# A FiLM layer on one core: loads on one queue, whole-slab stores, a narrow transposing matmul, compute in program order

## The chip, the cores and the metric

One core of a Trainium2 chip. The metric is device time in microseconds (us) of one execution. The profile's span is the time from the core's first to its last instruction; it is some 1.8 us shorter than the time (82.6 against 84.35 us in the profiled run of the kernel before). An execution counts as slow when it is more than 1.5% above the fastest of the same kernel. Comparisons use the others, the fast ones.

## The reference, cut to what matters

```python
x            : float32 [32, 512, 256]      # 16.78 MB in, 16.78 MB out
conditioning : float32 [32, 64]
gamma_proj, beta_proj : float32 [64, 256]

gamma = conditioning @ gamma_proj
beta  = conditioning @ beta_proj
return x * (1 + gamma[:, None, :]) + beta[:, None, :]
```

The arithmetic is two operations per element. The 33.69 MB of traffic cannot be reduced, since input and output are float32.

## The kernel before

x is cut into four slabs of 4 MB. A slab has eight batches on 128 partitions; each partition holds 32 rows of 1 KB, 32 KB in one contiguous run of memory. The kernel keeps all four slabs on the chip at once (four tiles of 32 KB per partition), so no buffer is reused. A matmul with a repeated identity turns the conditioning over and repeats each batch 16 times; a second matmul per slab gives gamma and beta for each partition. VectorE then handles 11 of every 16 rows and GpSimd 5, each with a multiply and an add, and each group of 16 rows is stored as soon as it is done.

```python
    cond_s = consts.tile([batch, cond_dim], f32)
    nc.scalar.dma_start(out=cond_s, in_=conditioning)          # small loads: ScalarE's queue
    gbproj = consts.tile([cond_dim, 2 * dim], f32)
    nc.scalar.dma_start(out=gbproj[:, :dim], in_=gamma_proj)
    nc.scalar.dma_start(out=gbproj[:, dim:], in_=beta_proj)
    for s in range(SLABS):                                     # slab loads: SP's queue
        ...
        for n in LOADS.get(s, [ROWS]):                         # slab 0: 8 + 24 rows, others 32
            nc.sync.dma_start(out=xs[:, r : r + n, :], in_=x_v[s, :, r : r + n, :])
    ...                                                        # rident: identity, each column 16 times
    nc.tensor.matmul(cond_T_p, lhsT=cond_s, rhs=rident, start=True, stop=True)   # 512 columns
    nc.vector.tensor_copy(out=cond_T, in_=cond_T_p)
    ...                                                        # per slab: gb_p = cond_T.T @ gbproj, copy to gb_s
    for s in range(SLABS):
        ...
        for r0 in range(0, ROWS, GROUP):                       # GROUP = 16, ON_DVE = 11
            ...
            nc.vector.scalar_tensor_tensor(out=v, in0=rows(g_p, nv), scalar=1.0, in1=v,
                                           op0=ALU.add, op1=ALU.mult)
            nc.gpsimd.tensor_tensor(out=w, in0=w, in1=rows(g_s, nw), op=ALU.mult)
            nc.vector.tensor_add(out=v, in0=v, in1=rows(b_p, nv))
            nc.gpsimd.tensor_tensor(out=w, in0=w, in1=rows(b_s, nw), op=ALU.add)
            nc.scalar.dma_start(out=o_v[s, :, r0 : r0 + GROUP, :],
                                in_=xs[:, r0 : r0 + GROUP, :])
```

## Time and profile before

| | kernel before |
|---|---|
| time, median of the first 3 runs | 85.82 us (84.4, 85.82, 86.3) |
| time of the profiled run, its span | 84.35 us, 82.6 us |
| VectorE busy, GpSimd busy | 49.9 us (60%), 46.2 us (56%) |
| DMA queues' packets, share of 16 engines' span | 48.6% + 48.0% |
| first multiply on VectorE, last compute ends | 17.5 us, 66.6 us |

The prediction below shows the lines of these views. In them PE is TensorE (PEld its weight loads), DVE is VectorE, ACT is ScalarE, POOL is GpSimd and SP is SyncE; q1 and q10 are the two DMA queues, and a packet is one contiguous run that one of the 16 DMA engines moves (the stores of the kernel before left 1024 records of 16 KB), or the 4 B record of a completion, 16 for each transfer. Three more things help in reading them. The DMA row gives the busy share of 40 equal slices of the span in tenths, 9 for full. Rows of the table by stretches end with the DMA share and the GB/s of that stretch; a packet is counted where it starts, so a share can pass 1.00 (1.30 from 4 to 6 us in the kernel before). And the chain of waits ends at the last instruction of an engine (66.6 us in the kernel before); a store that runs after it (until 81.4 us) is not part of it.

### The profile page before, as it was taken

How to read it: one execution, taken by the hardware profiler on the slowest of the kernel's cores; microseconds unless marked ns; L12 is line 12 of the kernel's file. 1: busy time of each engine (PE TensorE's matmuls, PEld its weight loads, DVE VectorE, ACT ScalarE, POOL GpSimd, SP SyncE). 2: the span in 40 equal slices, each digit the busy share in tenths (PEclk: the TensorE clock that was granted, in tenths of full speed). 3: DMA queues.
4: the chain of work that ended last, by engine and by line, in shares of the span. 5: the costliest groups of instructions: out<-in, count | busy, mean ns of one | idle time of the engine just before them, and what ended most of it. 6: DMA issues, size and time to landing. Idle time of an engine off the chain costs nothing.

```text
span 82.6 us, 156 instructions
## 1 busy us (share of the span) xinstructions
PE 9.1 (11%) x10; PEld 2.8 (3%) x10; DVE 49.9 (60%) x18; ACT 3.9 (5%) x9; POOL 46.2 (56%) x22
## 2 busy tenths in 40 slices
PE   0080000899600000000000000000000000000000
PEld 0100000443000000000000000000000000000000
DVE  2011000059999999999999999999999920000000
ACT  0600000034400000000000000000000000000000
POOL 2000000069999999999999999999995000000000
DMA  3899999969969989998889979899999999999992
GB/s 56 337 508 397 389 397 524 460 302 508 508 270 492 508 381 381 413 476 381 381 381 556 460 302 460 381 468 421 429 452 389 468 421 421 460 389 452 437 421 87
DMA packets 2080, 33.69 MB, mean 408 GB/s; under 512 B 288, under 2 KB 416, under 8 KB 416
## 3 DMA queue, kind: packets, MB, share of 16 engines
q1 hardware_dynamic: 720, 16.78, 48.6%
q10 hardware_dynamic: 1360, 16.92, 48.0%
HBM read 16.92 MB, written 16.78 MB: 408 GB/s over the span
## 4 chain that ended last, share of the span: by engine, by line
DVE 49%; DMA 16%; issue 11%; PE 2%; ACTq 1%; ACT 1%
DVE xs L100 30%; DVE xs L103 19%; DMA gbproj<-in_beta_proj_dram 16%; PE gb_p L79 2%; ACTq L50 1%; ACTq L48 0%; ACT gb_s L82 0%; ACT gb_s L85 0%
## 5 line engine op out<-in xcount | busy, mean ns | idle before, releaser
L102 POOL TENSOR_TENSOR xs<-xs,gb_s 128x1280 f32<-128x1280 f32 x8 | 23.0, 2895 | 16.2 <-ACT gb_s L82 16.2
L100 DVE SCALAR_TENSOR_TENSOR xs<-gb_p,xs 128x2816 f32<-128x2816 f32 x8 | 24.7, 3083 | 10.9 <-ACT gb_s L85 10.9
L103 DVE TENSOR_TENSOR xs<-xs,gb_p 128x2816 f32<-128x2816 f32 x8 | 24.7, 3086 | 0.3
L104 POOL TENSOR_TENSOR xs<-xs,gb_s 128x1280 f32<-128x1280 f32 x8 | 23.0, 2893 | 0.0
L79 PE MATMUL gb_p<-gbproj,cond_T 64*128 64x512 f32 x8 | 7.2, 1074 | 8.9 <-DMA gbproj<-in_beta_proj_dram 8.9
L74 DVE COPY cond_T<-cond_T_p 64x512 f32<-64x512 f32 x1 | 0.7, 683 | 4.3 <-PE cond_T_p L72 4.3
L79 PEld LDWEIGHTS gb_p<-gbproj,cond_T 64*128 64x128 f32 x8 | 2.5, 328 | 13.7 <-issue 13.7
L72 PE MATMUL cond_T_p<-rident,cond_s 32*64 32x512 f32 x2 | 1.9, 1065 | 3.9 <-DMA cond_s<-in_conditioning_dram 3.9
L82 ACT ACTIVATE gb_s<-gb_p 128x256 f32<-128x256 f32 x4 | 1.5, 383 | 16.4 <-PE gb_p L79 16.4
L85 ACT COPY gb_s<-gb_p 128x256 f32<-128x256 f32 x4 | 1.5, 367 | 0.0
L82 ACT ACT_TABLE_LOAD x1 | 1.3, 1283 | 2.4 <-issue 2.4
L67 DVE COPY rident<-ident 32x512 f32<-32x512 f32 x1 | 0.4, 416 | 1.2 <-POOL ident masks.py:199 1.2
L72 PEld LDWEIGHTS cond_T_p<-rident,cond_s 32*64 32x64 f32 x2 | 0.3, 202 | 3.9 <-issue 3.9
masks.py:197 POOL MEMSET ident<- 32x32 f32 x1 | 0.1, 114 | 0.3 <-POOLq L121 0.3
masks.py:199 POOL TENSOR_SCALAR_AFFINE_SELECT ident<-ident 32x32 f32<-32x32 f32 x1 | 0.2, 202 | 0.1
L121 POOL MEMSET const-float32-0.0<- 128x1 f32 x1 | 0.1, 103 | 0.2 <-issue 0.2
L121 POOL MEMSET const-bfloat16-1.0<- 128x1 bf16 x1 | 0.1, 106 | 0.0
L121 POOL MEMSET const-uint8-127<- 128x1 uint8 x1 | 0.1, 106 | 0.0
L121 POOL MEMSET const-float32-1.0<- 128x1 f32 x1 | 0.1, 103 | 0.0
## 6 DMA issues: line engine op xcount, KB each, us to landing
out_dram<-xs ACTq DMA_DIRECT2D x8, 2048.0 KB, 18.2
xs<-in_x_dram SPq DMA_DIRECT2D x3, 4096.0 KB, 32.9
xs<-in_x_dram SPq DMA_DIRECT2D x1, 3072.0 KB, 12.2
xs<-in_x_dram SPq DMA_DIRECT2D x1, 1024.0 KB, 4.6
gbproj<-in_gamma_proj_dram ACTq DMA_DIRECT2D x1, 64.0 KB, 9.1
gbproj<-in_beta_proj_dram ACTq DMA_DIRECT2D x1, 64.0 KB, 12.9
cond_s<-in_conditioning_dram ACTq DMA_DIRECT2D x1, 8.0 KB, 3.0
```

The lines of the kernel that those rows point to most:

```text
L50: nc.scalar.dma_start(out=gbproj[:, :dim], in_=gamma_proj)
L67: nc.vector.tensor_copy(out=rident.rearrange("p (b g) -> p b g", g=REP), in_=ident.to_broadcast([batch, batch, REP]),)
L72: nc.tensor.matmul(cond_T_p, lhsT=cond_s, rhs=rident, start=True, stop=True)
L74: nc.vector.tensor_copy(out=cond_T, in_=cond_T_p)
L79: nc.tensor.matmul(p_t, lhsT=cond_T[:, s * P : (s + 1) * P], rhs=gbproj, start=True, stop=True)
L82: nc.scalar.activation(out=s_t[:, :dim], in_=p_t[:, :dim], func=mybir.ActivationFunctionType.Identity, bias=1.0, scale=1.0)
L85: nc.scalar.copy(out=s_t[:, dim:], in_=p_t[:, dim:])
L100: nc.vector.scalar_tensor_tensor(out=v, in0=rows(g_p, nv), scalar=1.0, in1=v, op0=ALU.add, op1=ALU.mult)
L102: nc.gpsimd.tensor_tensor(out=w, in0=w, in1=rows(g_s, nw), op=ALU.mult)
L103: nc.vector.tensor_add(out=v, in0=v, in1=rows(b_p, nv))
L104: nc.gpsimd.tensor_tensor(out=w, in0=w, in1=rows(b_s, nw), op=ALU.add)
L121: nc = _bacc.Bacc("TRN2", target_bir_lowering=False, num_devices=1)
```

## The change: its intent, and the diff

The small loads leave ScalarE's queue and go behind slab 0 in SP's, so that they take no turns with it. Each slab is stored in one transfer with runs of 32 KB, as long as those of the loads. The transposing matmul works on 32 columns, and the repetition moves to a broadcasting copy per slab. The compute loop is issued in program order.

```diff
-    nc.scalar.dma_start(out=cond_s, in_=conditioning)
-    nc.scalar.dma_start(out=gbproj[:, :dim], in_=gamma_proj)
-    nc.scalar.dma_start(out=gbproj[:, dim:], in_=beta_proj)
 ...
+    load(nc.sync, 0, 0)
+    load(nc.sync, 0, 1)
+    nc.sync.dma_start(out=cond_s, in_=conditioning)
+    nc.sync.dma_start(out=gbproj[:, :dim], in_=gamma_proj)
+    nc.sync.dma_start(out=gbproj[:, dim:], in_=beta_proj)
+    load(nc.sync, 1, 0)
+    load(nc.sync, 2, 0)
+    load(nc.sync, 3, 0)
 ...
-    cond_T_p = psum.tile([cond_dim, batch * REP], f32)
-    nc.tensor.matmul(cond_T_p, lhsT=cond_s, rhs=rident, start=True, stop=True)
-    nc.vector.tensor_copy(out=cond_T, in_=cond_T_p)
+    cond_T_p = psum.tile([cond_dim, batch], f32)
+    nc.tensor.matmul(cond_T_p, lhsT=cond_s, rhs=ident, start=True, stop=True)
     for s, sl in enumerate(slabs):
+        nc.vector.tensor_copy(
+            out=c_t.rearrange("p (b g) -> p b g", g=rep),
+            in_=cond_T_p[:, b0 : b0 + n].to_broadcast([cond_dim, n, rep]),
+        )
 ...
+    STORES = [[32], [32], [32], [32]]
+    PIECE, ON_DVE = 16, 11
+    with tc.manual_schedule():
+        for s, sl in enumerate(slabs):
             ...                                   # the four operations of each piece as before
-            nc.scalar.dma_start(out=o_v[s, :, r0 : r0 + GROUP, :],
-                                in_=xs[:, r0 : r0 + GROUP, :])
+                nc.scalar.dma_start(out=sl["dst"][:, done : done + n, :],
+                                    in_=xs[:, done : done + n, :])
```

More of the change, by code (lines that the diff above doesn't have):

```diff
@@ L28 @@
     P = 128
-    SLABS = 4
-    BS = batch // SLABS
-    REP = P // BS
-    ROWS = BS * seq // P
-    assert SLABS * BS == batch and REP * BS == P and ROWS * REP == seq
-    x_v = x.flatten_outer_dims().rearrange("(s p r) d -> s p r d", s=SLABS, p=P)
-    o_v = out.flatten_outer_dims().rearrange("(s p r) d -> s p r d", s=SLABS, p=P)
-    LOADS = {0: [8, 24]}
-    GROUP = 16
-    ON_DVE = 11
+    SLABS = [(8, [8, 24]), (8, [32]), (8, [32]), (8, [32])]
+    assert sum(n for n, _ in SLABS) == batch
+    STORES = [[32], [32], [32], [32]]
+    PIECE, ON_DVE = 16, 11
+    x_f = x.flatten_outer_dims()
+    o_f = out.flatten_outer_dims()
     consts = ctx.enter_context(tc.tile_pool(name="consts", bufs=1))
@@ L44 @@
     psum = ctx.enter_context(tc.tile_pool(name="psum", bufs=1, space=bass.MemoryType.PSUM))
+    slabs = []
+    b0 = 0
+    for s, (n, loads) in enumerate(SLABS):
+        assert P % n == 0
+        rows = n * seq // P
+        r0, r1 = b0 * seq, (b0 + n) * seq
+        slabs.append(dict(
+            n=n, b0=b0, rows=rows, loads=loads,
+            src=x_f[r0:r1, :].rearrange("(p r) d -> p r d", p=P),
+            dst=o_f[r0:r1, :].rearrange("(p r) d -> p r d", p=P),
+            xs=xpool.tile([P, rows, dim], f32, name=f"xs{s}"),
+        ))
+        b0 += n
@@ L47, with load @@
+    def load(eng, s, i):
+        sl = slabs[s]
+        r = sum(sl["loads"][:i])
+        n = sl["loads"][i]
+        eng.dma_start(out=sl["xs"][:, r : r + n, :], in_=sl["src"][:, r : r + n, :])
     cond_s = consts.tile([batch, cond_dim], f32)
-    nc.scalar.dma_start(out=cond_s, in_=conditioning)
     gbproj = consts.tile([cond_dim, 2 * dim], f32)
-    nc.scalar.dma_start(out=gbproj[:, :dim], in_=gamma_proj)
-    nc.scalar.dma_start(out=gbproj[:, dim:], in_=beta_proj)
-    slabs = []
-    for s in range(SLABS):
-        xs = xpool.tile([P, ROWS, dim], f32, name=f"xs{s}")
-        slabs.append(xs)
-        r = 0
-        for n in LOADS.get(s, [ROWS]):
-            nc.sync.dma_start(out=xs[:, r : r + n, :], in_=x_v[s, :, r : r + n, :])
-            r += n
-        assert r == ROWS
+    load(nc.sync, 0, 0)
@@ L64 @@
+    load(nc.sync, 0, 1)
[5 more added lines that the diff above has]
+    load(nc.sync, 3, 0)
     ident = consts.tile([batch, batch], f32)
     make_identity(nc, ident)
-    rident = consts.tile([batch, batch * REP], f32)
-    nc.vector.tensor_copy(
-        out=rident.rearrange("p (b g) -> p b g", g=REP),
-        in_=ident.to_broadcast([batch, batch, REP]),
-    )
@@ L71 @@
-    cond_T_p = psum.tile([cond_dim, batch * REP], f32)
-    nc.tensor.matmul(cond_T_p, lhsT=cond_s, rhs=rident, start=True, stop=True)
-    cond_T = consts.tile([cond_dim, batch * REP], f32)
-    nc.vector.tensor_copy(out=cond_T, in_=cond_T_p)
-    gb_p, gb_s = [], []
-    for s in range(SLABS):
+    gb_p, gb_s = [], []
+    cond_T_p = psum.tile([cond_dim, batch], f32)
+    nc.tensor.matmul(cond_T_p, lhsT=cond_s, rhs=ident, start=True, stop=True)
+    for s, sl in enumerate(slabs):
+        n, b0 = sl["n"], sl["b0"]
+        rep = P // n
+        c_t = consts.tile([cond_dim, P], f32, name=f"cond_T{s}")
+        nc.vector.tensor_copy(
+            out=c_t.rearrange("p (b g) -> p b g", g=rep),
+            in_=cond_T_p[:, b0 : b0 + n].to_broadcast([cond_dim, n, rep]),
+        )
@@ L78 @@
         p_t = psum.tile([P, 2 * dim], f32, name=f"gb_p{s}")
-        nc.tensor.matmul(p_t, lhsT=cond_T[:, s * P : (s + 1) * P], rhs=gbproj,
-                         start=True, stop=True)
+        nc.tensor.matmul(p_t, lhsT=c_t, rhs=gbproj, start=True, stop=True)
         s_t = consts.tile([P, 2 * dim], f32, name=f"gb_s{s}")
@@ L87, with spread @@
         gb_s.append(s_t)
-    def rows(t, n):
+    def spread(t, n):
         return bass.AP(tensor=t.tensor, offset=t.offset, ap=[t.ap[0], [0, n], t.ap[1]])
-    for s in range(SLABS):
-        xs = slabs[s]
-        g_p, b_p = gb_p[s][:, :dim], gb_p[s][:, dim:]
-        g_s, b_s = gb_s[s][:, :dim], gb_s[s][:, dim:]
-        for r0 in range(0, ROWS, GROUP):
-            v = xs[:, r0 : r0 + ON_DVE, :]
-            w = xs[:, r0 + ON_DVE : r0 + GROUP, :]
-            nv, nw = ON_DVE, GROUP - ON_DVE
-            nc.vector.scalar_tensor_tensor(out=v, in0=rows(g_p, nv), scalar=1.0, in1=v,
-                                           op0=ALU.add, op1=ALU.mult)
-            nc.gpsimd.tensor_tensor(out=w, in0=w, in1=rows(g_s, nw), op=ALU.mult)
-            nc.vector.tensor_add(out=v, in0=v, in1=rows(b_p, nv))
-            nc.gpsimd.tensor_tensor(out=w, in0=w, in1=rows(b_s, nw), op=ALU.add)
-            nc.scalar.dma_start(out=o_v[s, :, r0 : r0 + GROUP, :],
-                                in_=xs[:, r0 : r0 + GROUP, :])
+    with tc.manual_schedule():
+        for s, sl in enumerate(slabs):
+            xs = sl["xs"]
+            g_p, b_p = gb_p[s][:, :dim], gb_p[s][:, dim:]
+            g_s, b_s = gb_s[s][:, :dim], gb_s[s][:, dim:]
+            done = 0
+            for n in STORES[s]:
+                for q0 in range(done, done + n, PIECE):
+                    nv, nw = ON_DVE, PIECE - ON_DVE
+                    v = xs[:, q0 : q0 + nv, :]
+                    w = xs[:, q0 + nv : q0 + PIECE, :]
+                    nc.vector.scalar_tensor_tensor(out=v, in0=spread(g_p, nv), scalar=1.0, in1=v,
+                                                   op0=ALU.add, op1=ALU.mult)
+                    nc.gpsimd.tensor_tensor(out=w, in0=w, in1=spread(g_s, nw), op=ALU.mult)
+                    nc.vector.tensor_add(out=v, in0=v, in1=spread(b_p, nv))
+                    nc.gpsimd.tensor_tensor(out=w, in0=w, in1=spread(b_s, nw), op=ALU.add)
+                nc.scalar.dma_start(out=sl["dst"][:, done : done + n, :],
+                                    in_=xs[:, done : done + n, :])
+                done += n
+            assert done == sl["rows"]
 _INS = ['x', 'conditioning', 'gamma_proj', 'beta_proj']
```

## The prediction

> **What bounds the kernel now.** I read the head of the profile page first: busy shares, then the slices, then the queues.
>
> ```profile
> PE 9.1 (11%) x10; PEld 2.8 (3%) x10; DVE 49.9 (60%) x18; ACT 3.9 (5%) x9; POOL 46.2 (56%) x22
> ...
> DMA  3899999969969989998889979899999999999992
> ...
> q1 hardware_dynamic: 720, 16.78, 48.6%
> q10 hardware_dynamic: 1360, 16.92, 48.0%
> HBM read 16.92 MB, written 16.78 MB: 408 GB/s over the span
> ```
>
> No compute engine is above 60%. The two DMA queues together take 48.6 + 48.0 = 96.6% of the 16 DMA engines' span, 79.8 of 82.6 us, and the DMA row is full from its second slice to its last but one. The queues are told apart by bytes: q1 carries the 16.78 MB of x, and q10, the queue that ScalarE issues on, the stores and the small loads. The 2.8 us outside are the ends: by the packet records the first packet starts at 1.7 us and the last ends at 81.4 us.
>
> The chain of waits seems to say otherwise, so I read it with its last entries.
>
> ```profile
> DVE 49%; DMA 16%; issue 11%; PE 2%; ACTq 1%; ACT 1%
> ```
> ```profile
> 60.46 3.01 DVE xs L100
> 63.47 0.02 issue
> 63.49 3.09 DVE xs L103
> ```
>
> It names VectorE for half the span. But it follows back from the last compute instruction, which ends at 66.6 us. The last 16 us have no compute in them, so the chain does not explain them. The table by stretches shows what does.
>
> ```profile
> 14.60:26.00 11.40, 7.16 (x8) 2.50 (x8) 8.45 (x3) 2.59 (x8) 8.70 (x4) 1.00 0.97 420
> 26.00:50.00 24.00, 0.00 (x0) 0.00 (x0) 23.86 (x9) 0.00 (x0) 24.00 (x9) 1.00 1.00 423
> 50.00:66.00 16.00, 0.00 (x0) 0.00 (x0) 15.89 (x6) 0.00 (x0) 12.97 (x5) 1.00 1.01 434
> 66.00:80.50 14.50, 0.00 (x0) 0.00 (x0) 0.58 (x1) 0.00 (x0) 0.00 (x0) 1.00 1.00 429
> ```
>
> The last two columns are DMA share and GB/s. Loads only, the mix, and stores only, with compute beside them or without: 420 to 434 GB/s and a share of 0.97 or more in every row. **The bound is the transport of 33.69 MB**, and compute only has to hand stores over before the queue runs dry.
>
> [...] In the stretch with both kinds, 26 to 50 us, I read the two queue lines:
>
> ```profile
> q1 hardware_dynamic: 238, 6.75, 67.0%
> q10 hardware_dynamic: 224, 3.41, 33.1%
> ```
>
> Packets come nearly one for one, but a load packet is 32 KB and a store packet 16 KB, so loads get two thirds. [...]
>
> **The change, part by part.**
>
> *Stores in 32 KB runs.* Packet records: an 8 KB load takes 309 ns, a 16 KB store 611 ns, a 32 KB load 1213 ns (medians). Twice 611 is 1222, so joining two runs saves 9 ns. The 1024 store packets are 64 on each of 16 engines, 32 pairs: 32 x 9 ns = 0.29 us. Four completion packets fewer per engine at 9 ns: 0.04 us. Together **-0.3 us**, on the bounding resource.
>
> *Small loads behind slab 0.* Bytes and packets are the same; per engine some 0.5 us (8 packets of 46 ns, 2 of 18 ns, completions) move within the queue, **0 us** in transport. Now the wait for them:
>
> ```profile
> 1.72 12.90 DMA gbproj<-in_beta_proj_dram
> 14.62 0.14 issue
> 14.76 2.06 PE gb_p L79 x2
> 16.82 0.02 issue
> 16.84 0.38 ACT gb_s L82
> 17.22 0.27 ACT gb_s L85
> ```
>
> Today beta takes 12.9 us although it was issued at 1.7 us, since each little packet takes turns with a slab packet: its last data packet ends at 12.8 us, about when slab 0's do (12.75). Behind slab 0 in one queue I expect the data at about 12.9 us and the wait over at 13.5 us (conditioning's wait ended 0.7 us after its last packet), 1.1 us earlier. But conditioning now comes with it, so the transpose, hidden before, is exposed.
>
> *Narrow matmul.* Two passes of 512 columns at 1065 ns become two of 32: in proportion 0.07 us each, with fixed costs I guess 0.3 us for both. The 0.42 us copy of the repeated identity goes; the 0.68 us copy becomes four of a quarter of its width, 0.2 us each, of which one is on the path. Exposed: some 0.6 us less 0.4 us that overlaps with the wait for beta. So VectorE starts near 16.7 us instead of 17.5: **-0.8 us, off the bound**.
>
> *Program order, one store per slab.* Scheduling moves no bytes. VectorE's pace stays 6.13 us per piece (eight pieces from 17.52 to 66.58). The first store goes out after two pieces, at about 16.7 + 12.3 = 29 us instead of 25.9. Until then the load queue keeps the DMA engines full: only 13.5 of the 24 big load packets per engine had been done when the first store packet started today (29.8 us). **0 us**.
>
> Sum: -0.3 us of 82.6, or 85.82 x (82.3 / 82.6) = 85.5 us. All that could be won, ends included, is small: per engine 8 x 309 + 8 x 923.5 (24 KB packets) + 24 x 1213 + 64 x 611 ns + 0.55 us of small ones = 78.6 us, against 79.8 us taken. Even the full 1.2 us of slowed packets plus 0.3 would be 1.8%.
>
> **Rivals.**
> *A new wait for slab 3.* With equal runs, loads get half of the engines where they had two thirds. The first store was issued at 25.9 us and its packets started at 29.8; the same lag puts store packets at about 33 us after the change, with (33 - 13) / 1.27 = 15.7 big load packets done (1.27 us each in the load-only stretch). The other 8.3 alternate with stores at 1.24 + 1.21 us: the loads end at 53 us, landing 1 us later at 54; with no such lag, 56.5. VectorE wants slab 3 at 16.7 + 6 x 6.13 = 53.5 us. So I expect a stall of 0.5 to 3 us, new, and hidden if the next rival fails.
>
> *The last store comes too late.* It is 4 MB now: 8 packets x 1.213 = 9.7 us per engine, plus about 1 us from issue to first packet. The work before it ends at 81.4 - 9.7 = 71.7 us, so it may be issued as late as 70.7. VectorE would end at 16.7 + 49.1 + 0.5 to 3 = 66.3 to 68.8 us. The slack is 2 to 4 us; today it is larger, since the last store is half as long. If it were overrun by 2 us the time would be 87.5 us.
>
> *A real gain on the DMA side.* Large runs, or fewer takings of turns, could take away the slowed load packets (1.24 to 1.27 against 1.213 us) and the first slab's slow start. For it: the trace has them. Against it: they are there in loads without any small packets or stores beside them. Worth at most 1.2 us: 84.3 us.
>
> **Range and chances.** The centre is 85.5, moved to 85.3 for the third rival, which I find likelier than the second. The runs of before spread from 84.4 to 86.3, wider than every effect above, so the range is 83.9 to 86.8. Faster by 2% needs under 84.1, more than all the slack in the sum, so chiefly a lucky median: 0.13. Slower by 2% needs over 87.5, an overrun of the last store: 0.07. Within 2%: 0.80.
>
> **What would show it.** Right: queue shares again near 97% together, stretches at 420 to 434 GB/s, store packets half as many, byte shares near 50:50 where loads and stores mix, VectorE starting near 16.7 us, a wait of VectorE or GpSimd for the load of x before slab 3, and a DMA row full to the end. Wrong: empty tenths in the DMA row between two stores, a first multiply later than 18 us, a wait of over 4 us for x, or a rate clearly above 434 GB/s.

## The result, and the profile after

The changed kernel took 84.53 us (median of 6 runs, 84.45 to 84.78). The kernel before took 85.2 us (median of 6 runs, 84.4 to 86.47). A ratio is the mean time of one kernel's fast runs over that of the other's of the same rounds, so not quite the ratio of these medians: it is **1.0004, with a 95% interval of 0.9985 to 1.0024, the same**. The medians differ because three of the six runs of the kernel before were slow (85.82, 86.3, 86.47); its other three, 84.4 to 84.59, lie where the changed kernel's do.

The head of the page after the change, with busy shares, slices and queues (q1 is now every load, q10 every store):

```profile
PE 7.6 (9%) x10; PEld 2.8 (3%) x10; DVE 49.7 (60%) x20; ACT 3.9 (5%) x9; POOL 46.6 (56%) x22
...
DMA  2898989889969989979969998996998899799790
...
q1 hardware_dynamic: 928, 16.92, 49.1%
q10 hardware_dynamic: 576, 16.78, 47.0%
```

The same engines are as busy as before and the DMA row has no hole. The stores have fallen from 1024 data packets to 512, and the two shares together from 96.6 to 96.1%, which is 0.3 us of packet time, as predicted. The span did not follow: 82.7 us against 82.6.

The table by stretches after the change (engine times, then clock, DMA share and GB/s), for the same four stretches as before:

```profile
14.60:26.00 11.40, 7.00 (x8) 2.31 (x8) 9.11 (x5) 2.59 (x8) 8.87 (x4) 1.00 0.96 414
26.00:50.00 24.00, 0.00 (x0) 0.00 (x0) 23.86 (x9) 0.00 (x0) 23.68 (x9) 1.00 1.03 437
50.00:66.00 16.00, 0.00 (x0) 0.00 (x0) 15.89 (x6) 0.00 (x0) 13.52 (x5) 1.00 0.99 426
66.00:80.50 14.50, 0.00 (x0) 0.00 (x0) 0.27 (x1) 0.00 (x0) 0.00 (x0) 1.00 1.00 434
```

Each rate differs from the one before by 5 to 14 GB/s up or down, and the four stretches together moved 28.3 MB against 28.1: I read the differences as the edges of 32 KB packets, not as a new rate.

The two queues after the change, while loads and stores run side by side (33 to 50 us):

```profile
q1 hardware_dynamic: 112, 3.67, 49.9%
q10 hardware_dynamic: 112, 3.67, 49.9%
```

Packets are one for one as before, and with equal runs the bytes are too, where loads had two thirds. The chain of waits shows the start of the compute (start, length, what):

```profile
1.64 11.87 DMA cond_s<-in_conditioning_dram
...
13.64 0.40 PE cond_T_p L81 x2
...
14.06 0.29 DVE cond_T L86
...
14.40 2.09 PE gb_p L91 x2
...
17.19 3.10 DVE xs L114
```

The waits for the small loads end at 13.5 us for conditioning and at 13.9 for beta (14.6 before), but the transpose now lies open behind conditioning: 0.76 us from its first matmul to the first gb_p. The multiply starts at 17.2 us, 0.3 us earlier than before. The first store is issued at 29.6 us instead of 25.9, its packets start at 33.7, and a new wait has come, in the table of waits (in total, times, longest):

```profile
POOL xs L116 <- DMA xs<-in_x_dram: 0.8, 1, 0.8
```

It is GpSimd waiting for slab 3 at 52 us. VectorE, which is 1.2 us later there, does not wait.

### The profile page after: what moved, and what is told of

It reads as the page before. It is cut to its first block, busy times and chain, and to the rows that moved or that the text cites. A ratio compares the mean times of both kernels' runs of the same rounds, so it can differ in the third digit from the quotient of the medians.

```text
span 82.7 us, 151 instructions
## 1 busy us (share of the span) xinstructions
PE 7.6 (9%) x10; PEld 2.8 (3%) x10; DVE 49.7 (60%) x20; ACT 3.9 (5%) x9; POOL 46.6 (56%) x22
## 2 busy tenths in 40 slices
DMA packets 1504, 33.69 MB, mean 407 GB/s; under 512 B 224, under 2 KB 352, under 8 KB 352
## 4 chain that ended last, share of the span: by engine, by line
DVE 51%; DMA 14%; issue 9%; PE 3%; SPq 1%; ACT 1%
DVE xs L114 30%; DVE xs L117 21%; DMA cond_s<-in_conditioning_dram 14%; PE gb_p L91 3%; SPq L63 1%; PE cond_T_p L81 0%; ACT gb_s L93 0%; DVE cond_T L86 0%; ACT gb_s L96 0%
## 5 line engine op out<-in xcount | busy, mean ns | idle before, releaser
L86 DVE COPY cond_T<-cond_T_p 64x128 f32<-64x128 f32 x4 | 0.9, 274 | 14.1 <-PE cond_T_p L81 14.1
```

The costliest lines, as they stand in the source:

```text
L86: nc.vector.tensor_copy(out=c_t.rearrange("p (b g) -> p b g", g=rep), in_=cond_T_p[:, b0 : b0 + n].to_broadcast([cond_dim, n, rep]),)
```

## The experiments

Theory: the 33.69 MB set the time, so a part counts only if it changes what the 16 engines move, delays their first packet, or lets them run dry. Rivals: the VectorE chain that the profile names sets the end; or each packet has a fixed cost worth saving. The twelve kernels ran each beside fresh runs of the kernel before.

| run | what | median us | ratio to before (95%) |
|---|---|---|---|
| e1_copy | changed, no arithmetic on x | 84.91 | 1.0046 (1.0019 to 1.0073) |
| e2_run4k | changed, stores in 4 KB runs | 85.62 | 1.0128 (1.0106 to 1.0150) |
| e3_run1k | changed, stores in 1 KB runs | 89.4 | 1.0574 (1.0550 to 1.0597) |
| e4_st16 | changed, two 16 KB stores per slab | 84.4 | 0.9987 (0.9966 to 1.0008) |
| e5_after_d2 | changed, last store 5.9 us later | 86.2 | 1.0200 (1.0182 to 1.0218) |
| e6_after_d3 | changed, last store 8.9 us later | 89.36 | 1.0570 (1.0552 to 1.0588) |
| e7_before_d3 | before, last store 8.7 us later | 85.59 (2 of 4 slow; fast: 84.61, 84.69) | 1.0014 (0.9993 to 1.0036) |
| e8_small_act | changed, small loads first on ScalarE | 84.67 (1 of 4 slow) | 1.0013 (0.9995 to 1.0031) |
| e9_before_behind | before, small loads behind slab 0 | 84.63 | 1.0012 (0.9993 to 1.0031) |
| e10_before_sp_first | before, small loads first on SP | 86.09 | 1.0184 (1.0166 to 1.0203) |
| e11_after_again | the changed kernel | 84.66 (1 of 6 slow) | 1.0019 (0.9993 to 1.0045) |
| e12_sixteen | changed, sixteen transfers | 84.37 | 0.9979 (0.9965 to 0.9994) |

### Does compute set the end? (e1_copy)

```diff
-                for q0 in range(done, done + n, PIECE):
-                    ...                          # all four operations on x
                 nc.scalar.dma_start(out=sl["dst"][:, done : done + n, :], ...)
```

> The changed kernel with its arithmetic on x left out (result wrong on purpose); stores depend on the loads alone. Theory (transport bound, 33.69 MB[...] between a head of 1.7 us and a tail of 1.2 to 1.4 us): the span stays at 82 to 83 us, a ratio of 0.99 to 1.01 to the kernel before, although VectorE and GpSimd lose 46 to 49 us of work. Rival (the chain of waits through VectorE, half of the span, sets the end): well under 80 us.

By its packet records the kernel before moved the 33.69 MB between 1.7 and 81.4 us, at 423 GB/s, in a span of 82.6 us.

The result is wrong on purpose: x is copied. The head of its page:

```profile
span 83.0 us, 101 instructions
...
PE 7.6 (9%) x10; PEld 2.8 (3%) x10; DVE 0.9 (1%) x4; ACT 3.9 (5%) x9; POOL 0.5 (1%) x6
```

VectorE fell from 49.7 to 0.9 us and GpSimd from 46.6 to 0.5, and the kernel was not faster at all; it was 0.5% slower than the kernel before. The VectorE half of the chain of waits is worth nothing in time.

### What does a packet cost? (e2_run4k, e3_run1k, e4_st16)

```diff
-                nc.scalar.dma_start(out=sl["dst"][:, done : done + n, :],
-                                    in_=xs[:, done : done + n, :])
+                d_r = sl["dst"].rearrange("p (c two k) d -> p two c (k d)", two=2, k=RUN)   # RUN = 4 or 1
+                x_r = xs.rearrange("p (c two k) d -> p two c (k d)", two=2, k=RUN)
+                for h in range(2):
+                    nc.scalar.dma_start(out=d_r[:, h], in_=x_r[:, h])
```

> The changed kernel with each slab's store cut into two DMAs of interleaved 4 KB runs: 256 store packets per engine in place of 32. Prediction's term (9 ns of fixed cost per packet on the bounding engines): 224 x 9 ns = +2.0 us. Rival (the 9 ns in the packet records lie over the neighbouring packet and cost nothing): within 0.4 us of the changed kernel.

> The same with runs of 1 KB: 1024 store packets per engine in place of 32. Prediction's term: 992 x 9 ns = +8.9 us, over 93 us. Rival (overlapped, no cost): within 0.6 us. Something between: a cost that appears only when packets are short.

Neither theory hit. Against the changed kernel's 84.53 us, 224 more packets per engine cost 1.09 us and 992 more cost 4.87 us: **4.9 ns per packet both times**, a little over half of the 9 ns that the packet records suggested. One caution: these two kernels have sixteen transfers and the changed kernel twelve, and the last experiment shows that twelve cost 0.25 us more at the end. Adding it makes 6.0 and 5.2 ns of the two figures. The comparison free of it is between these two kernels: 89.4 - 85.62 = 3.78 us for 768 packets, again 4.9 ns. The traces agree. While stores ran alone they moved 386 GB/s in 1 KB runs (e3_run1k, 46 to 84 us) and 422 in 4 KB runs (e2_run4k, 46 to 80 us), which is 42.4 and 155.3 ns per packet on each of 16 engines. The difference, 112.9 ns for 3 KB, is 37.6 ns for each KB (the records of the kernel before give the same: 1213 - 611 = 602 ns for 16 KB), and taking that off leaves some 4.8 ns per packet.

The records say 46 and 159 ns for the same packets, since neighbouring packets of an engine overlap in them. The queue shares of e3_run1k show it:

```profile
q10 hardware_dynamic: 16512, 16.78, 53.8%
q1 hardware_dynamic: 928, 16.92, 46.7%
```

They sum to 100.5% of the span, 88.1 us per engine, although only 84.7 us lie between the first packet and the last. So a packet's recorded time is longer than what it adds to the queue.

```diff
-    STORES = [[32], [32], [32], [32]]
+    STORES = [[16, 16]] * 4
```

> The changed kernel with two stores of 16 KB runs per slab, as before. Prediction's term: +0.3 us. Rival (overlapped): 0.0 us. Either way the first store should be issued near 23 to 24 us, loads should again get two thirds of the bytes while both kinds run, and the GpSimd wait for slab 3 (0.8 us) should go without moving the end.

The ratio to the kernel before is 0.9987, the median 0.13 us below the changed kernel's: end to end, 32 KB runs give no gain over 16 KB runs. (This kernel has sixteen transfers too, so what its 36 more packets per engine cost, 0.18 us at 4.9 ns, would be hidden by the 0.25 us.) The first store was issued at 23.0 us, the GpSimd wait for slab 3 is gone from the table of waits, and the queues between 28 and 48 us are two to one again:

```profile
q1 hardware_dynamic: 188, 5.64, 66.6%
q10 hardware_dynamic: 191, 2.87, 33.5%
```

### How late may the stores be? (e5_after_d2, e6_after_d3, e7_before_d3)

```diff
+    scratch = consts.tile([P, ON_DVE, dim], f32, name="scratch")
+    nc.vector.memset(scratch, 1.0)
     with tc.manual_schedule():
+        for _ in range(DELAY):                   # 2 or 3; 3 in the kernel before
+            nc.vector.scalar_tensor_tensor(out=scratch, in0=spread(gb_p[0][:, :dim], ON_DVE), scalar=1.0,
+                                           in1=scratch, op0=ALU.add, op1=ALU.mult)
```

> The changed kernel with two extra VectorE operations of 3.09 us on a scratch tile ahead of its first multiply: every store goes out 6.2 us later. Theory: today the last store is issued at 66.4 us, its 9.7 us of packets must begin by 81.3 - 9.7 = 71.6 us, so with about 1 us from issue to first packet the slack is 4.2 us; 6.2 us overrun it by 2.0 us, a time of about 86.5 us, with empty tenths in the DMA row just before the last store. Rival (VectorE chain sets the end): +6.2 us. Rival (stores have more slack than I think): +0.

> The same with three, 9.3 us later. Theory: slack overrun by 5.1 us, about 89.6 us, 3.1 us more than with two (beyond the slack every us counts in full). Rival (chain): +9.3 us.

> The kernel before with the same three extra operations, 9.3 us later. Theory: its last store is half as long (4.9 us of packets), so it may be issued as late as 81.4 - 4.9 - 1 = 75.5 us; it is issued at 66.7 + 9.3 = 76.0 us: overrun by 0.5 us only, a ratio of about 1.006, where the changed kernel with the same delay loses some 5 us. So the change would have spent 4 to 5 us of unseen slack. Rival (both kernels have the same slack): the same loss in both.

The theory holds closely. Slack is how much later the last store may be issued before the time grows. The traces give the real delay; these lines are the stores of the changed kernel, of e5_after_d2 and of e6_after_d3, then of the kernel before and of e7_before_d3 (first issue, time from it to the end of the last issue):

```profile
29.61 37.08 ACTq L119 DMA_DIRECT2D out_dram<-xs  x4
35.49 37.07 ACTq L125 DMA_DIRECT2D out_dram<-xs  x4
38.49 37.08 ACTq L125 DMA_DIRECT2D out_dram<-xs  x4
25.94 41.06 ACTq L105 DMA_DIRECT2D out_dram<-xs  x8
33.23 42.43 ACTq L112 DMA_DIRECT2D out_dram<-xs  x8
```

So the last store went out 5.9 and 8.9 us later, not the nominal 6.2 and 9.3. Two extra operations cost 86.2 - 84.53 = 1.67 us, three cost 4.83 us; the third cost its 3.0 us in full. The changed kernel's slack is therefore 5.9 - 1.7 = 4.2 us, and 8.9 - 4.8 = 4.1 us from the other run; 4.2 was estimated beforehand. The stretches of e6_after_d3 show the hole:

```profile
68.00:72.00 4.00, 0.00 (x0) 0.00 (x0) 4.00 (x2) 0.00 (x0) 0.00 (x0) 1.00 0.91 393
72.00:76.00 4.00, 0.00 (x0) 0.00 (x0) 3.12 (x2) 0.00 (x0) 0.00 (x0) 1.00 0.31 131
76.00:80.00 4.00, 0.00 (x0) 0.00 (x0) 0.00 (x0) 0.00 (x0) 0.00 (x0) 1.00 1.22 524
```

The earlier stores are done at 73.7 us, VectorE ends at 75.1, and the first packet of the last store starts at 76.1. The kernel before took the same three operations with a ratio of 1.0014, from two fast runs. In its trace, which is of a slow run, the last store was issued at 75.3 us instead of 66.7, so the slack before is about 8.7 us or more (8.8 by the estimate). The change at least halves that slack, and no time of the two kernels themselves shows it.

### Does the place of the small loads matter? (e8_small_act, e9_before_behind, e10_before_sp_first)

```diff
 e8: changed kernel
+    nc.scalar.dma_start(...)   # conditioning, gamma, beta on ScalarE, ahead of the slab loads
 e9: kernel before
+    nc.sync.dma_start(...)     # the three on SP, behind slab 0
 e10: kernel before
+    nc.sync.dma_start(...)     # the three on SP, ahead of slab 0
```

> The changed kernel with the three small loads back on ScalarE's queue and ahead of the slab loads, as before. Theory (the place of the small loads moves no bytes): time within 0.3 us of the changed kernel, the first multiply of VectorE within 1 us of 17.2 us. Rival (their interleaving with the slab packets is what made three of six runs of the kernel before take 85.8 to 86.5 us instead of 84.4 to 84.6): runs near 86 us come back in this kernel and not in the others of this call that keep the small loads behind the slab.

> The kernel before with one part of the change alone: the three small loads issued by SP behind slab 0; stores of 16 KB runs, wide transposing matmul and scheduling as before. Theory for the fast runs (no bytes moved): a ratio of 0.997 to 1.003. For the slower executions near 86.5 us: so far 7 of 28 executions with the small loads on ScalarE's queue beside slab 0, 0 of 30 with them behind it. If that placement is what matters, none of the 6 executions here is above 86 us; if the slower executions fall on any kernel alike (7 of 58 overall), one is likely here too.

> The kernel before with the three small loads issued by SP ahead of slab 0, in the one queue, so that nothing takes turns with the slab. They should land near 4 us and VectorE's first multiply start when the first 8 KB per partition and the matmuls are there, at some 6 to 8 us, ten us earlier than before. Theory (transport bound): the fast runs stay within 0.5% of the kernel before all the same. Rival (compute chain): some 9 us faster. Slower executions: none if taking turns with the slab is what matters.

ScalarE's queue or behind slab 0 makes no difference in fast runs: 1.0013 and 1.0012. In e9_before_behind the wide transpose lies open behind the small loads and VectorE starts at 19.1 us, 1.6 us later than in the kernel before; that cost nothing either. Ahead of slab 0 on the same engine costs 1.8%, which I had not expected. Its first two stretches:

```profile
0.00:2.00 2.00, 0.00 (x0) 0.00 (x0) 0.41 (x1) 1.26 (x1) 0.53 (x6) 1.00 0.02 4
2.00:4.00 2.00, 1.59 (x2) 0.28 (x2) 0.00 (x0) 0.02 (x1) 0.00 (x0) 1.00 0.52 119
```

SP needs 0.38 + 0.52 + 0.58 us to issue the three small loads, so the first slab load is issued at 2.4 us instead of 0.7. The DMA engines have next to nothing until then (the kernel before had shares of 0.29 and 0.84 in these stretches), and the delay of 1.6 us comes out at the end as 86.09 - 84.49 = 1.6 us. The first gb_p matmul started at 5.1 us, nearly ten us earlier, but my expectation of a first multiply at 6 to 8 us was wrong too: it came at 14.7 us, 2.8 us earlier than in the kernel before, since its 11 rows reach into the second load of slab 0, which landed at 14.6. The table of waits:

```profile
DVE xs L100 <- DMA xs<-in_x_dram: 11.2, 2, 9.7
```

So this run doesn't test the compute chain; e1_copy does. The place behind slab 0 earns something only against the place ahead of it on the same engine; the kernel before avoided that cost in another way, by issuing from ScalarE.

### The slow runs (e8_small_act, e9_before_behind, e11_after_again)

> The changed kernel again, beside the two above on the same chip. Theory: ratio of fast runs 0.998 to 1.003, no execution above 85 us.

The idea that only the small loads' turns with slab 0 cause the slow runs fell. One of the six runs of e11_after_again took 86.52 us, and it was the profiled one. The stretch from 14 to 33 us, in that run and then in the fast profile of the same kernel:

```profile
14.00:33.00 19.00, 7.19 (x8) 2.47 (x8) 16.65 (x10) 2.59 (x8) 16.13 (x6) 1.00 0.97 362
```
```profile
14.00:33.00 19.00, 7.22 (x9) 2.50 (x8) 16.58 (x10) 2.59 (x8) 15.79 (x6) 1.00 1.03 435
```

While loads run alone, all their 32 KB packets take about 1396 ns instead of 1213 in the slow run, on the same program; once stores are beside them, they are back at 1213 to 1216. The slow profile of e7_before_d3 shows it too, with 1353 to 1361 ns. Counting all runs, slow ones were 10 of 50 with the small loads taking turns with slab 0 (42 of the kernel before, 4 each of e7 and e8), and 1 of 48 with them behind it (and 0 of 4 of e10, ahead of it). That may be a tendency, but the chips differ as well (on one chip, 0 of 7 runs of the kernel before were slow). No run tested the obvious rival, that something outside the program was using the same memory at the time. What starts it stays open.

### Where the small gain went (e12_sixteen)

At 4.9 ns, 36 packets fewer per engine (32 data, 4 completions) should still give 0.18 us. In the two traces the last packet did end earlier, at 81.30 us against 81.39, but the program ended later. (One trace each does not measure so small a gain: with the same store packets it was 81.42 us in e8_small_act and 81.43 in e12_sixteen.) The record of SyncE's last waits shows why it ended later. The last store lands 0.35 us after its last packet in both kernels. In the kernel before, SyncE then has one wait left. In the changed kernel it steps through five (start us, semaphores):

```
81.666 S[103] S[101]      <- the last store's semaphore
81.734 S[104] S[100]
81.793 S[105] S[107]
81.855 S[109] S[106]
81.914 S[110] S[108]
```

The transfers take their semaphores in turn, and with twelve transfers the last store has an early one. From landing to the end of the program it is 0.83 us before and 1.08 us after. All fourteen traces fall in these two groups: 0.83 us in the eight with sixteen transfers, 1.08 to 1.09 us in the six with twelve.

```diff
-    SLABS = [(8, [8, 24]), ...]
+    SLABS = [(8, [8, 8, 16]), ...]
+    # conditioning, gamma and beta each in two halves: 16 transfers instead of 12
```

> The changed kernel with the same whole-slab stores but sixteen transfers in all instead of twelve (slab 0 loaded in three pieces, the small loads halved), so that its last store completes on the semaphore that SyncE waits for last. In the four traces looked at, the end of the program comes 0.83 us after the last store has landed with sixteen transfers and 1.08 us after it with twelve, where SyncE still steps through four more waits of some 0.06 us each that are met already. If those steps are where the gain of the joined stores was given back: 0.83 us from landing to end, a span near 82.5 us, a ratio to the kernel before of about 0.997. Rival (the last 32 KB packets themselves make the end later): still 1.08 us. Transport is the same in both, so nothing more is to be won.

The landing came at 81.79 us and the end at 82.61: 0.83 us, as expected. The ratio is 0.9979, the only one of all runs whose interval lies below 1. It is the best version found, by 0.2%. That the tail was worth 0.25 us is shown; that the rest of the gain is the saved packets fits the 0.18 us, but is within the noise of any one pair of runs.

## Why the prediction was right, and where its working was not

**The bound: right.** Transport sets the time; e1_copy shows it, and the two queue shares near 97% were the right thing to read. The full stretches were at 414 to 437 GB/s after the change and at 420 to 434 before it, the same within the edges of packets.

**Stores in 32 KB runs, -0.3 us: mis-sized.** The step took the 9 ns by which two 16 KB records exceed one 32 KB record as time on the engines. The runs measured 4.9 ns per packet, 0.18 us for this change, and 0.25 us was added in SyncE's last waits, which the prediction did not reckon with. The packet sum fell by the predicted 0.3 us; the span did not.

**The small loads: the data as predicted, the wait too short.** The data were expected at about 12.9 us, and the last data packet ended at 12.8. But the wait for beta ended at 13.9 us and not at 13.5, 1.1 us after that packet where the prediction took some 0.6 us, going by conditioning in the kernel before. The overlap of 0.4 us came (conditioning at 13.5, beta at 13.9), but some 0.35 us of the transpose stayed exposed in place of 0.2. So the multiply, expected at 16.7 us, started at 17.2. It was off the bound, so without effect, as e8 and e9 show. In a passage now cut, the prediction also inferred that the move to SP saves issue time. It only moved it: the three issues took 0.40 + 0.51 + 0.61 us on ScalarE before and 0.42 + 0.52 + 0.61 us on SP after (1.64 to 3.32 us with the gaps), ahead of the load of slab 1. Behind slab 0 that is hidden; e10 shows it ahead of slab 0.

**A new wait for slab 3: half right.** The sum gave 0.5 to 3 us to VectorE, which did not wait: the last packet of the slab loads ended at 51.0 us where 53 was reckoned, since 17 of the 24 load packets per engine were done when the stores came, not 15.7. The 0.8 us measured fell on GpSimd, which was ahead of VectorE; the list of signs names GpSimd too, but the sum does not. It was hidden. **The last store too late: rightly rejected**, with a slack of 4.2 us by e5 and e6 where 2 to 4 were estimated; the low end came from the stall of VectorE that did not happen. **A real gain on the DMA side: did not come.** By the packet records, what exceeds the shortest time of each size sums to some 1.2 us per engine before and 1.3 after.

**The centre of 85.3 us was 0.8 too high**, which lies in its starting figure. I multiplied a ratio onto a median of 85.82 us, two of whose three runs were slow; the profile beside it was of a run of 84.35. From that run the same sum, 82.3 / 82.6, would have given 84.0 us, too low by the 0.3 us that did not come and by the spread of the runs. What was right for its reasons is "within 2%"; that 84.53 lies within 83.9 to 86.8 owes much to the width of the range, which the slow runs had set.

## What to carry to other kernels

When the DMA queues are full from start to end, ask of each part of a change only whether it alters the bytes, the first packet or the chance of running dry, and check the last with a delay put in on purpose: a change that costs no time may have spent half of the slack. Issue the large load first on its engine: in e10 the 1.6 us of issues ahead of it were added to the end in full. And start a prediction from the state of the profiled run, not from a median of mixed states.

## What the traces show besides

- Where two queues had packets waiting, the turns went by whole contiguous runs. In the changed kernel 16 store packets of 32 KB started from 33.7 us on (as many as there are engines), 16 load packets from 34.9, 16 store packets from 36.2, and so on, with 112 against 112 from 33 to 50 us. In e4_st16, from 28 to 48 us, it was 188 load packets of 32 KB against 191 store packets of 16 KB, completions included (66.6% to 33.5% of the time). In the kernel before, 16 small packets of 1 KB and 16 slab packets of 24 KB started every 0.95 us (three such rounds from 5.6 to 8 us).
- The first store waited while the loads filled the engines: 4.1 us from its issue to its first packet (29.6 to 33.7 us; 25.9 to 29.8 us in the kernel before), against about 1 us with idle engines (0.7 to 1.7 us at the start).
